# Which engine waits for the last store: TensorE or SyncE at the end of an add-and-GELU kernel

## The chip, the cores and the metric

The kernel runs on one core of one Trainium2 chip. The core has five engines, each with an instruction queue of its own: TensorE (PE in the profile), VectorE (DVE), ScalarE (ACT), GpSimd (POOL) and SyncE (SP). [...] The metric is the device time of one execution in microseconds (us); lower is better.

## The reference

The kernel adds two arrays of 1024 x 4096 float32 values and passes the sum through the tanh form of GELU:

```python
def reference(x, y):
    z = x + y
    return (0.5 * z * (1 + np.tanh(np.sqrt(2 / np.pi) * (z + 0.044715 * z ** 3)))).astype(np.float32)
```

It reads 33.55 MB and writes 16.78 MB.

## The kernel before, in words

Each of the 128 partitions holds 32,768 consecutive elements of x, y and the output. SyncE issues all transfers: four loads of x and four of y, of 8,192 elements a partition each, in turn (lines 129 and 136), and then three stores of 16,384, 10,240 and 6,144 elements a partition (line 140). The arithmetic runs in 16 chunks of 2,048 elements a partition. GpSimd adds x and y in all chunks but the first (line 153). ScalarE squares (line 158), VectorE forms the cubic term (line 164), ScalarE takes a sigmoid (line 169) and VectorE multiplies (line 176) into the tile that is stored. TensorE has no arithmetic at all. The order in each queue is written out by hand in four lists, and `tc.compile()` on line 231 adds waits, branches and the end of the program.

Two helpers then edit the compiled program. `begin_early` moves the first two loads ahead of the barrier at the start. `wait_late` edits the last block. As compiled, that block begins with SyncE waiting for everything that is outstanding; then comes a barrier of all five engines, then GpSimd clears the kernel's semaphores (line 50), then a second barrier. Each barrier is made of two semaphores, 96 and 97: every engine but GpSimd raises 96 in a DRAIN instruction, GpSimd waits for four of those, adds 4 to 97, and every other engine takes one off 97 in an EVENT_SEMAPHORE instruction. All of these instructions carry line 231 in the profile.

`wait_late` takes the wait for the last store (semaphore 103, which the last store raises to 32) out of SyncE's first wait. It leaves semaphore 103 out of GpSimd's clearing, by splitting the range in two, and appends one more EVENT_SEMAPHORE after the second barrier. That instruction waits until semaphore 103 is at least 32 and subtracts 32. In the kernel before it stands in SyncE's queue as its last instruction. So the barriers and the clearing run while the last store is still moving, and the program's own last instruction is SyncE's. Behind the last instruction of each queue follow instructions that are not the kernel's: they have no line in the profile, but the trace holds their updates of semaphores.

Of the kernel before, what the change touches and what calls it, by code (L numbers as in the profile page):

```python
# [25 lines left out]
def wait_late(nc):  # L26

    body, end = (b.instructions for b in nc.main_func.blocks[1:3])  # L30
    last = [i for i in body if isinstance(i, mybir.InstDMACopy)][-1]
    (sem,) = [u.id for u in last.sync_info.on_update]
    all_done = end[0]
    reset = next(i for i in end if isinstance(i, mybir.InstDrain) and i.is_reset_sema)
    at = end.index(reset)
    clear = end[at + 1]
    first, stop = reset.reset_range_start, reset.reset_range_stop
    assert all_done.engine == mybir.EngineType.SP and reset.engine == mybir.EngineType.Pool
    assert isinstance(clear, mybir.InstISA) and clear.engine == mybir.EngineType.Pool
    waits = all_done.sync_info.on_wait  # L40
    (its,) = [w for w in waits if w.id == sem]

    end[0] = mybir.InstDrain(
        name=all_done.name, engine=all_done.engine, debug=all_done.debug, is_reset_sema=False,
        sync_info=mybir.SyncInfo(on_wait=[w for w in waits if w.id != sem], on_update=[]),
    )
    parts = []
    for f, e in ((first, sem), (sem + 1, stop)):
        if f < e:
            nc.gpsimd.sem_clear(range(f, e))  # L50
            parts.append(nc.cur_bb.bb.instructions.pop())
    end[at + 1 : at + 2] = parts
    end.append(
        mybir.InstEventSemaphore(
            name=clear.name, engine=mybir.EngineType.SP, debug=clear.debug,
            sync_info=mybir.SyncInfo(
                on_wait=[its],
                on_update=[
                    mybir.SyncUpdate(
                        sync_type="semaphore", id=sem, ant_name=its.ant_name,  # L60
                        update_mode="sem-sub-imm", update_value=its.wait_value,
                    )
                ],
            ),
        )
    )
# [3 lines left out]
def kernel(  # L70
# [160 lines left out]
    tc.compile()  # L231
    begin_early(nc, 2)
    wait_late(nc)


# [28 lines left out]
```

## Time and profile before

| what | value |
|---|---|
| median of 3 runs | 120.31 us (120.29 to 120.6) |
| the profiled execution's own time | 120.49 us |
| span of the profile, first to last instruction of the kernel | 118.8 us (118.83) |
| time of the profiled execution outside the span | 1.66 us (120.49 - 118.83) |
| busy in the span | DVE 73.7 us, ACT 61.0 us, POOL 69.7 us, TensorE none |
| traffic | 50.33 MB, mean 424 GB/s over the span |
| last store issued by SyncE | starts at 106.9 us, 3,072 KB, 11.9 us to landing |
| the kernel's last instruction | SyncE's EVENT_SEMAPHORE, starts at 118.8 us, 17 ns |

Times within the profile count from the start of the span. A "q" behind an engine's name (SPq, POOLq) stands for instructions that its sequencer handles alone: waits, drains, issues of transfers. TensorE's appear as PEq or PEldq. Such instructions are not counted as busy. The duration shown for one of them mostly begins when its wait is over, so a short duration doesn't mean that it waited briefly.

### The profile page before, as it was taken

Reading aid. Unit: us, or ns where it says so; the run is one execution under the profiler, and the core shown is the slowest. Engines: PE = TensorE matmul, PEld = TensorE weight load, DVE = VectorE, ACT = ScalarE, POOL = GpSimd, SP = SyncE. Lnnn points to the kernel's source line nnn. Section 1 sums busy time; section 2 is a strip of 40 time slices with the busy share of each in tenths; the row PEclk is TensorE's granted clock in tenths of the full one; section 3 lists DMA queues with packets and bytes.
Section 4 is the critical chain, followed back from the end, with each engine's and each line's share of the span. In section 5 each row is a group of like instructions: output and inputs, shape, how many; then the busy total and the mean of one; then the engine's idle time right before and its main releaser. Section 6 shows DMA issues by size and latency. Waiting matters only on the chain.

```text
span 118.8 us, 172 instructions
## 1 busy us (share of the span) xinstructions
DVE 73.7 (62%) x35; ACT 61.0 (51%) x34; POOL 69.7 (59%) x19
## 2 busy tenths in 40 slices
DVE  0000000635799995739999968999994999990000
ACT  5000000063888965197698647888839779810000
POOL 0000000699996099999959999959999990000000
DMA  7989898989999898989899898998899889999996
GB/s 243 463 375 507 353 529 353 507 375 474 408 419 463 375 507 353 518 364 496 386 452 430 386 496 353 529 529 353 353 596 463 353 353 441 441 441 441 397 397 265
DMA packets 1584, 50.33 MB, mean 424 GB/s; under 512 B 176, under 2 KB 176, under 8 KB 176
## 3 DMA queue, kind: packets, MB, share of 16 engines
q1 hardware_dynamic: 1584, 50.33, 98.7%
HBM read 33.55 MB, written 16.78 MB: 424 GB/s over the span
## 4 chain that ended last, share of the span: by engine, by line
DMA 51%; POOL 26%; POOLq 4%; DVE 4%; DVEq 2%; ACT 2%; issue 0%; SPq 0%
DMA y<-in_y_dram 51%; POOL z L153 26%; POOLq L231 4%; DVE w L164 2%; DVEq L231 2%; DVE z L176 2%; ACT w L158 2%; SPq L129 0%; POOLq L153 0%
## 5 line engine op out<-in xcount | busy, mean ns | idle before, releaser
L153 POOL TENSOR_TENSOR z<-z,y 128x2048 f32<-128x2048 f32 x15 | 69.4, 4660 | 28.3 <-DMA y<-in_y_dram 28.3
L158 ACT ACTIVATE w<-z 128x2048 f32<-128x2048 f32 x16 | 30.1, 1882 | 37.7 <-DVE z L153 21.5
L164 DVE SCALAR_TENSOR_TENSOR w<-w,z 128x2048 f32<-128x2048 f32 x16 | 36.7, 2296 | 11.2 <-ACT w L158 11.0
L176 DVE TENSOR_TENSOR z<-w,z 128x2048 f32<-128x2048 f32 (+1 forms) x17 | 35.9, 2155 | 0.0
L169 ACT ACTIVATE w<-w 128x2048 f32<-128x2048 f32 x16 | 29.7, 1855 | 4.4 <-DVE w L164 4.3
L153 DVE TENSOR_TENSOR z<-z,y 128x2048 f32<-128x2048 f32 x1 | 2.3, 2293 | 20.5 <-DMA y<-in_y_dram 20.5
L216 ACT ACT_TABLE_LOAD x1 | 1.3, 1283 | 1.3 <-PEq L248 1.3
L215 DVE MEMSET one<- 128x1 f32 x1 | 0.1, 59 | 1.3 <-PEq L248 1.3
L248 POOL MEMSET const-float32-0.0<- 128x1 f32 x1 | 0.1, 98 | 0.2 <-issue 0.2
L216 ACT ACTIVATE one<-one 128x1 f32<-128x1 f32 x1 | 0.2, 203 | 0.0
L248 POOL MEMSET const-bfloat16-1.0<- 128x1 bf16 x1 | 0.1, 101 | 0.0
L248 POOL MEMSET const-uint8-127<- 128x1 uint8 x1 | 0.1, 101 | 0.0
L248 POOL MEMSET const-float32-1.0<- 128x1 f32 x1 | 0.1, 98 | 0.0
## 6 DMA issues: line engine op xcount, KB each, us to landing
z<-in_x_dram SPq DMA_DIRECT2D x4, 4096.0 KB, 31.4
y<-in_y_dram SPq DMA_DIRECT2D x4, 4096.0 KB, 22.2
out_dram<-z SPq DMA_DIRECT2D x1, 5120.0 KB, 15.8
out_dram<-z SPq DMA_DIRECT2D x1, 3072.0 KB, 11.9
out_dram<-z SPq DMA_DIRECT2D x1, 22.0
```

Source lines behind the costliest of these rows:

```text
L153: eng.tensor_add(out=zt[:, a:b], in0=zt[:, a:b], in1=yt[s][:, o : o + b - a])
L158: nc.scalar.activation(out=wt[c], in_=zt[:, a:b], func=act.Square, scale=root)
L164: nc.vector.scalar_tensor_tensor(out=wt[c], in0=wt[c], scalar=c1, in1=zt[:, a:b], op0=alu.add, op1=alu.mult)
L169: nc.scalar.activation(out=wt[c], in_=wt[c], func=act.Sigmoid)
L176: ins = nc.vector.tensor_mul(out=zt[:, a + o : a + o + n], in0=wt[c][:, o : o + n], in1=zt[:, a + o : a + o + n],)
L215: nc.vector.memset(one, 0.0)
L216: nc.scalar.activation(out=one, in_=one, func=act.Sigmoid)
L231: tc.compile()
L248: nc = _bacc.Bacc("TRN2", target_bir_lowering=False, num_devices=1)
```

## The change

The instruction that waits for semaphore 103 and subtracts 32 from it is placed in TensorE's queue and not in SyncE's. It stays the last instruction of the block, with the same wait and the same subtraction. SyncE's queue then ends with its step of the second barrier, and TensorE's queue has one instruction more behind its own step of that barrier. Nothing else differs: all loads, stores and arithmetic stand in the same order on every engine.

```diff
     end.append(
         mybir.InstEventSemaphore(
-            name=clear.name, engine=mybir.EngineType.SP, debug=clear.debug,
+            name=clear.name, engine=mybir.EngineType.PE, debug=clear.debug,
             sync_info=mybir.SyncInfo(
                 on_wait=[its],
                 on_update=[
```

## The prediction

> **What bounds the kernel now.** I first read the page's slices, to see what the stretch around the change is limited by:
>
> ```profile
> DVE  0000000635799995739999968999994999990000
> POOL 0000000699996099999959999959999990000000
> DMA  7989898989999898989899898998899889999996
> ```
>
> The DMA engines are busy from the first slice to the last, and no engine computes in the last four slices (from about 107 us). The end is the last store. SyncE's waits in the stretch from 107 us on say who waits for it:
>
> ```profile
> SPq L140 <- DVE z L176: 10.7, 1, 10.7
> SPq L231 <- SPq L231: 6.4, 1, 6.4
> SPq L231 <- DMA out_dram<-z: 4.2, 1, 4.2
> ```
>
> The columns are us in total, times and longest. The last store is issued after the last multiplication of VectorE (first row). SyncE then waits 4.2 us for the store before the last, passes both barriers, and waits 6.4 us more. The view puts this last wait down to SyncE itself, but the instruction waits for semaphore 103 alone, so it is the last store that ends it. Then I read what the instructions of line 231 cost each engine, in the view of that line for 110 to 119 us:
>
> ```profile
> L231 SPq EVENT_SEMAPHORE  x6: 17/22/4230, 107.3 to 118.8; - x6
> L231 ACTq EVENT_SEMAPHORE  x2: 17/17/17, 111.9 to 112.4; - x2
> L231 DVEq EVENT_SEMAPHORE  x2: 21/21/21, 111.9 to 112.4; - x2
> L231 PEldq EVENT_SEMAPHORE  x2: 51/51/51, 111.9 to 112.5; - x2
> ```
>
> The numbers after the count are shortest, median and longest in ns, then the first and last start. The reader should see two things. The same kind of instruction takes 17 ns on SyncE (its shortest, the moved one among them) and 51 ns on TensorE. And everything but SyncE's last instruction is over at 112.5 us, 6.3 us before the end at 118.8 us.
>
> The profile's instructions stop there, but 1.66 us of this execution's 120.49 lie outside its span, and the trace keeps updates of semaphores from them. Those of semaphore 2, in us from the start of the span, are:
>
> ```
> before the kernel   -0.374 -0.340 -0.302 -0.258 -0.235 | -0.123 -0.084 -0.050 -0.003
> first after it     112.736 112.770 112.975 113.019 118.971 | 119.015 119.053 119.087 119.135
> second after it    119.922 119.956 119.995 120.039 120.062 | 120.161 120.199 120.233 120.280
> ```
>
> Nine updates make one pass over the five engines, up and down again. In the first pass after the kernel, four updates are made long before the end, then nothing for 6 us, then the fifth 0.141 us after SyncE's last instruction. So SyncE is fifth, the turning point, and the other four have already taken their upward step when the store lands. The change removes this arrangement.
>
> [...] the second pass takes 120.280 - 119.922 = 0.358 us. [...]
>
> **Where TensorE stands in the pass.** No record names the engine of an update, so I infer it. Before the kernel the last update is at -0.003 us, and TensorE's first instruction is the last of all, at 0.312 us; VectorE, ScalarE and GpSimd begin between 0.119 and 0.131, SyncE at 0. In the reset between the two later passes, semaphores are cleared in groups of 51. The first group (3 to 53) ends last, at 119.698, at about 7.6 ns each even after the others are through, where the first clears of SyncE's group take about 1.5 ns each. The slow sequencer of the table above is TensorE's. I take TensorE as first in the pass: it goes up first and comes down last.
>
> **The change part by part.**
>
> Removed: SyncE's last instruction and what follows it up to the barrier. Semaphore 103 got its last increment at 118.796, the instruction began at 118.813 (17 ns later) and took 17, and SyncE's update came at 118.971. From the landing to the turning point: 118.971 - 118.796 = 0.175 us. From there down to the first engine: 119.135 - 118.971 = 0.164. Sum: 0.339 us.
>
> Added: the same instruction on TensorE.
> - Waking: in both barriers TensorE began 28 and 29 ns after semaphore 97 was raised, SyncE 17. I take 0.028.
> - Executing: 0.051, from the row above. Subtracting 32 and not 1 should cost the same: SyncE's last instruction takes 17 ns like its decrements.
> - From its last kernel instruction to its step in the pass: TensorE's last ended at 112.501, the first update came at 112.736: 0.235. SyncE needs 0.141. I take 0.235 unchanged. It could be less if some of it was waiting for others; I bound it from below by SyncE's 0.141.
> - The whole pass, since nobody can go up before TensorE: the second pass is a case of just that, with TensorE last out of its reset. It takes 0.358.
>
> Sum: 0.028 + 0.051 + 0.235 + 0.358 = 0.672 us from the landing to the end of the pass. Difference: 0.672 - 0.339 = **+0.333 us**. Nothing hides it: at that point no transfer and no arithmetic is left. From the pass on, reset and second pass follow as before: TensorE's reset was last before and is last again.
>
> Moved with it: nothing else. No DMA is issued in that block, and SyncE's three stores stand ahead of it in the same order. Queued behind the waiting instruction on TensorE is nothing of the kernel, only its part of the end sequence, and all other engines wait for that in the pass. SyncE passes 6.3 us earlier to its own step, where it waits for the other four; I cost that at nothing, since the pass is held by TensorE in any case. The GpSimd clearing, leaving out semaphore 103, is as before.
>
> So the span itself should grow hardly at all: the kernel's last instruction ends at 118.796 + 0.028 + 0.051 = 118.875 and not 118.830, +0.045 us. The time outside it should grow from 1.66 to about 1.66 + 0.29 = 1.95 us. For the profiled execution: 120.49 + 0.33 = 120.82. That one lies 0.18 above the median of the runs shown, within their 0.31 us of spread, so for the median: 120.31 + 0.33 = **120.64 us**, +0.28%.
>
> A measurement of this kernel can tell about 0.3% from no change, 0.36 us here, so the forecast lies just under what counts as slower.
>
> **Rivals.**
>
> The pass is dearer than the second one shows. In the first pass the third step came 112.975 - 112.770 = 0.205 us after the second, where the warm passes show 0.038 and 0.039. I read that as an engine that arrived late. But if it is what this step costs after a kernel (GpSimd's last kernel instruction had ended at 112.413, the earliest of all, which speaks for it), the path is longer by 0.205 - 0.039 = 0.166: +0.50 us, 120.81. If, beyond that, instructions that each engine runs ahead of its step come into the path one after the other, up to 0.14 us for each of the four behind TensorE, it is +0.333 + 0.56 = +0.89, 121.20. Against it: they had 6 us to run ahead. Slower is certain once over 0.03 us is added to my sum.
>
> TensorE isn't first in the pass, but second to fourth. Then one to three of the upward hops (0.034, 0.039 and 0.044) fall away: +0.333 - 0.034 = 0.30 to 0.333 - 0.117 = 0.22 us; with the lower bound of 0.141 for its way to the pass also 0.094 less: +0.12, 120.43. The slow group of semaphores speaks against it.
>
> The other side, no loss or a gain: the measured end doesn't hang on TensorE's passing the barrier but on SyncE's own end sequence, which now lies under the store. Then SyncE's 0.141 goes and only TensorE's 0.045 comes: 0.045 - 0.141 = -0.10 us, 120.21. It decides if the records after the landing show SyncE's group going on early. Against it: 6 us of silence in the pass before the change, and none of it is skipped.
>
> That the change does nothing (another wait ends last) can be excluded: the moved instruction is the last of the span, 6.3 us behind all others.
>
> **How the numbers follow.** TensorE first, pass as in the second: 0.64; with some 0.1 us of scatter in the runs around +0.333, it gives slower 0.29, same 0.34, faster 0.01. Dearer pass: 0.18, all slower. TensorE elsewhere: 0.12, same 0.11, faster 0.01. End sequence of SyncE: 0.06, same 0.04, faster 0.02. Sum: slower 0.47, same 0.49, faster 0.04. The range begins between the cases +0.12 and +0.22 less a little scatter (120.40) and reaches over the dearer pass at 120.81 and some way towards 121.20, to 121.00; about 0.1 is left out on each side.
>
> **What would show it.** In the profile after: a span of 118.9 us if the DMA part is the same, ending with a TensorE EVENT_SEMAPHORE of 51 ns; no update of semaphore 2 between the barriers at 112.5 us and the landing; then nine updates in a row, the first 0.31 us after the last increment of semaphore 103, the ninth 0.36 later. Wrong would be early updates (TensorE isn't first), a pass well over 0.36 us (the dearer pass), or a first pass as short as before.

## The result and the profile after

The changed kernel takes 120.72 us (median of 6 runs, 120.67 to 120.79), the kernel before 120.39 us (median of 6, 120.29 to 120.6). The ratio is 1.0027, 95% interval 1.0014 to 1.0039: 0.33 us more, between 0.17 and 0.47 us. The change costs time, since the whole interval lies above 1, but it stays just under the 0.3% that the prediction took as the bound of a clear loss.

The page of the changed kernel has the same picture in its slices as before: transfers to the end, nothing computed in the last four slices.

```profile
DVE  0000000635799995749999958999994999990000
POOL 0000000699996199999959999959999990000000
DMA  7999898989999898989899898998899889999896
```

SyncE's waits from 107 us on (us in total, times, longest):

```profile
SPq L140 <- DVE z L176: 10.7, 1, 10.7
SPq L231 <- DMA out_dram<-z: 4.3, 1, 4.3
SPq L231 <- PEq L231: 0.6, 2, 0.5
```

The row of 6.4 us that stood between the first two is gone: SyncE waits for nothing more after the second barrier. (The third row, its waits in the barriers, is the same in the kernel before.) The view of line 231 for 110 to 119 us shows where the instruction went (count, then shortest, median and longest in ns, then the first and last start):

```profile
L231 SPq EVENT_SEMAPHORE  x5: 17/28/4252, 107.2 to 112.3; - x5
L231 PEldq EVENT_SEMAPHORE  x3: 51/51/51, 111.8 to 118.7; - x3
L231 ACTq EVENT_SEMAPHORE  x2: 17/17/17, 111.8 to 112.3; - x2
```

SyncE's are one fewer and end at 112.3; TensorE has one more, at 118.7 us, and it takes 51 ns. That one ends the span, at 118.705 us. The span is no longer than before (118.83), although the time is. The difference lies outside the span, in the updates of semaphore 2 (us from the start of the span; semaphore 103 had its last increment at 118.625):

```
first after the kernel   118.984 119.018 119.056 119.100 119.124 | 119.222 119.261 119.295 119.342
second after it          120.129 120.164 120.202 120.246 120.269 | 120.368 120.406 120.440 120.487
```

Before, four of the nine steps of the first pass were taken 6 us ahead of the landing. Now the first comes 0.359 us after the landing, and the other eight follow it. In the profiled executions the pass ends 0.339 us after the landing before and 0.717 after: 0.378 us more. The time outside the span (the time of a run less its span, mean of all runs; spans are on record to 0.1 us) rose from 1.663 us (35 runs of the kernel before, made with E1 to E4 below) to 1.995 us (6 runs), by 0.332. The span itself has 0.046 us more of TensorE's waking and executing, which the scatter of the spans covers (118.6 to 119.5 us in those 35 runs). The two add up to the 0.378 us of the traces.

### The profile page after: what moved, and what is told of

Read it like the earlier page. It is cut to its first block, busy times and chain, and to the rows that moved or that the text cites. A ratio compares the mean times of both kernels' runs of the same rounds, so it can differ in the third digit from the quotient of the medians.

```text
span 118.7 us, 172 instructions
## 1 busy us (share of the span) xinstructions
DVE 73.7 (62%) x35; ACT 61.0 (51%) x34; POOL 69.6 (59%) x19
## 4 chain that ended last, share of the span: by engine, by line
DMA 51%; POOL 26%; POOLq 4%; DVE 4%; DVEq 2%; ACT 2%; issue 0%; SPq 0%
DMA y<-in_y_dram 51%; POOL z L153 26%; POOLq L231 4%; DVE w L164 2%; DVEq L231 2%; DVE z L176 2%; ACT w L158 2%; SPq L129 0%; POOLq L153 0%
```

## The experiments

The theory: after the landing, four things follow each other. The waiting engine wakes; it executes the instruction; it makes its own way to its step in the pass (the time from the end of its last kernel instruction to that step); then comes the rest of the pass behind that step. The rivals: only TensorE's slow sequencer costs, with 51 ns for the instruction that takes SyncE 17 (A); any engine but SyncE, the turning point, pays the same (B); the end depends on SyncE's own end sequence. Two properties of the traces served as gauges: the number of updates of semaphore 2 made ahead of the landing (4 with SyncE, 0 with TensorE) is read as the waiting engine's place, and the distances between events give each part in ns. The columns from "wakes" to "sum" are in ns, from the profiled executions; "sum" is the time from the landing to the end of the first pass. "Outside" is the mean of time less span over the runs, in us. The ratio of an experiment is to runs of the kernel before made in the same round; their "outside" was 1.663 us for E1 to E4, 1.671 for E5 to E8 and 1.668 for E9 to E12.

| kernel | early steps | wakes | executes | way | rest of pass | sum | outside | ratio to before, 95% interval |
|---|---|---|---|---|---|---|---|---|
| before (SyncE) | 4 | 17 | 17 | 141 | 164 | 339 | 1.663 | |
| after (TensorE) | 0 | 29 | 51 | 279 | 358 | 717 | 1.995 | 1.0027 [1.0014, 1.0039] |
| E1 ScalarE | 1 | 21 | 17 | 140 | 324 | 502 | 1.640 | 0.9998 [0.9988, 1.0009] |
| E2 VectorE | 3 | 28 | 21 | 183 | 242 | 474 | 1.790 | 1.0021 [1.0013, 1.0030] |
| E3 GpSimd | 2 | 24 | 17 | 561 | 286 | 888 | 2.200 | 1.0044 [1.0032, 1.0056] |
| E4 TensorE and 4 drains | 0 | 28 | 51 + 364 | 192 | 358 | 993 | 1.906 | 1.0064 [1.0052, 1.0076] |
| E5 SyncE, 4 drains on TensorE | 4 | 17 | 17 | 140 | 164 | 338 | 1.663 | 1.0001 [0.9994, 1.0009] |
| E6 TensorE, 4 drains on SyncE | 0 | 29 | 51 | 279 | 359 | 718 | 2.010 | 1.0033 [1.0021, 1.0045] |
| E7 SyncE and 4 drains | 4 | 17 | 17 + 232 | 120 | 163 | 549 | 1.643 | 1.0021 [1.0014, 1.0029] |

In E4 and E7 the four drains belong to the span, so "outside" alone doesn't show them; the sum does.

**E1 to E3: another engine waits.** The edit, here for ScalarE (VectorE is `DVE`, GpSimd `Pool`):

```diff
-            name=clear.name, engine=mybir.EngineType.PE, debug=clear.debug,
+            name=clear.name, engine=mybir.EngineType.Activation, debug=clear.debug,
```

> The wait for the last store stands on ScalarE. From the landing (last increment of semaphore 103) to the end of the first pass it was 0.339 us with SyncE waiting and 0.717 with TensorE. Theory (each engine pays waking, executing, its own way to its step, and the rest of the pass behind its step): ScalarE is second, so one early update of semaphore 2, and 0.02 + 0.017 + way + (0.358 - 0.034), the way between SyncE's 0.141 and the 0.311 that the trace of before allows: 0.50 to 0.67 us, 0.16 to 0.33 over before. Rival A (only TensorE's slow sequencer costs): as before, within 0.05 us. Rival B (every engine but the turning point pays alike): +0.33 to 0.38.

> The wait for the last store stands on VectorE. Theory (waking, executing, own way, rest of the pass): VectorE is fourth, so three early updates, and 0.027 + 0.021 + way + (0.358 - 0.117), [...]: 0.47 to 0.84 us, 0.13 to 0.50 over before, the low end likelier. Rival A (only TensorE's slow sequencer costs): as before, within 0.05 us. Rival B (all but the turning point pay alike): +0.33 to 0.38.

> The wait for the last store stands on GpSimd. Theory (waking, executing, own way, rest of the pass): GpSimd is third, so two early updates, and 0.024 + 0.017 + way + (0.358 - 0.072), the way between 0.141 and the 0.562 us from GpSimd's last kernel instruction (112.413) to the late third update of before (112.975). If that late update was GpSimd's own way, 0.89 us, 0.55 over before, more than TensorE although it stands later; if it was a dear hop of the pass, TensorE waiting would have shown it too, and its pass took 0.358. Low end 0.47, +0.13. Rival A (only TensorE's slow sequencer costs): as before, within 0.05. Rival B (all but the turning point pay alike): +0.33 to 0.38.

The early steps are 1, 3 and 2, with 0 for TensorE and 4 for SyncE: the pass goes TensorE, ScalarE, GpSimd, VectorE, SyncE. That settles the places that the prediction had to infer. That the four updates behind the fifth go back the same way is still a reading: no record names an update's engine. In E3 the updates of the first pass are, in us from the start of the span, with the landing at 118.643 and the end of GpSimd's instruction at 118.684:

```
first after the kernel   112.619 112.653 119.245 119.290 119.313 | 119.411 119.450 119.485 119.531
```

Two steps are taken early, and the third comes 561 ns after GpSimd's instruction. In the kernel before it came 562 ns after GpSimd's last instruction (112.975 - 112.413). That decides between the two readings of the late third step there: it is GpSimd's own way, not a dear hop. So GpSimd costs 0.549 us over before by the trace and 0.53 us (0.39 to 0.67) in the runs, more than TensorE although it stands two places later. In the view of line 231 its instruction is no slower than SyncE's (first row before, second row E3):

```profile
L231 POOLq EVENT_SEMAPHORE  x4: 17/17/17, 111.8 to 112.4; - x4
L231 POOLq EVENT_SEMAPHORE  x5: 17/17/17, 111.7 to 118.7; - x5
```

The reader should see that the second row alone would have suggested a cost like SyncE's; what costs is behind the last instruction of the profile. A falls with VectorE and GpSimd, B with the spread from 0.135 (VectorE) to 0.549 us (GpSimd) by the trace. The low end of 0.47 us expected for VectorE was the author's estimate; the trace has 0.474. For VectorE the trace gives 0.135 us more than before, and outside the span the runs have 0.127; the ratio has slightly more, 0.16 to 0.36 us, the rest of it in spans that were 0.06 us longer on average. ScalarE doesn't fit: its trace gives 0.163 us more, its runs show no difference, and even the upper end of the interval, 0.11 us, is below. So for ScalarE the theory has the path right and the time wrong. E9 to E12 are about that.

**E4 to E7: four drains more, on the engine that waits and on one that doesn't.** The edit, here for TensorE, behind the last instruction of the changed kernel (E4) or of the kernel before (E5); with `SP` it gives E6 and E7:

```diff
+    more = [
+        mybir.InstDrain(
+            name=nc.get_next_instruction_name(), engine=mybir.EngineType.PE, debug=clear.debug,
+            is_reset_sema=False,
+            sync_info=mybir.SyncInfo(on_wait=[], on_update=[]),
+        )
+        for k in range(4)
+    ]
+    end.extend(more)
```

> The changed kernel with four DRAIN instructions more on TensorE behind the wait. Theory (all that TensorE has behind the wait is on the path, one after the other): a DRAIN takes 8 ns and began 100 ns after the instruction ahead of it, so 4 x 0.108 = 0.43 us more than the changed kernel: 0.717 + 0.43 = 1.15 us from the landing to the end of the pass, and 0.8 us (0.65%) over before. Rival (what is behind the wait is fetched and run ahead, only the wait itself counts): as the changed kernel, 0.717 and +0.3%.

> The kernel before (SyncE waits) with four DRAIN instructions more at the end of TensorE's queue. Theory (TensorE's way to its step lies under the store there): TensorE's step comes 0.43 us later, at about 113.2 us from the start of the span, 5.6 us ahead of the landing; from the landing to the end of the pass 0.339 us as before, time as before within 0.05 us. Rival (TensorE's end sequence counts wherever the wait stands): +0.4 us, +0.35%.

> The changed kernel with four DRAIN instructions more at the end of SyncE's queue. Theory: SyncE's way to its step is now under the store: as the changed kernel, 0.717 us from the landing to the end of the pass, +0.3% on before. Rival (SyncE's end sequence sets the end by itself): 4 x 0.055 = 0.22 us more, +0.5% on before.

> The kernel before with four DRAIN instructions more on SyncE behind the wait. Theory: SyncE's way is on the path there: a DRAIN of 7 ns with some 48 ns ahead of it, 4 x 0.055 = 0.22 us more, 0.56 us from the landing to the end of the pass, +0.18% on before. Rival (only TensorE's end sequence sets the end): as before.

The drains lengthen the path when they stand behind the wait on the waiting engine (E4: +0.276 us over the changed kernel; E7: +0.210 us over before) and cost nothing on an engine that doesn't wait (E5 and E6: 0.001 us or less by the traces). The rows of TensorE's drains in the changed kernel (first) and in E4, in which the added lines move 231 to 240:

```profile
L231 PEldq DRAIN  x1: 8/8/8, 112.0 to 112.0; - x1
L240 PEldq DRAIN  x5: 8/8/8, 112.1 to 119.2; - x5
L240 PEldq EVENT_SEMAPHORE  x3: 51/51/51, 112.0 to 118.8; - x3
```

Four drains of 8 ns take 364 ns, from the end of the wait to the end of the last: the time is between instructions, not in them. E4 stayed under the 0.43 us expected, since the drains began 116, 72 and 68 ns apart, not 108, and the way behind them shrank from 279 to 192 ns. The rival that what is behind the wait runs ahead is refuted by E4. That TensorE's end sequence counts wherever the wait stands is refuted by E5, that SyncE's sets the end by itself by E6, and that only TensorE's counts by E7.

**E8: one drain on TensorE, for its way.** The block above with `range(1)`, in the kernel before.

> The kernel before with one DRAIN more at the end of TensorE's queue, for what makes TensorE's way to its step 0.279 us with the change where it was 0.235 before. If one instruction more in TensorE's queue shifts what follows, the way from the end of the DRAIN to the first update is about 0.28; if it is the long wait, or the kind of the last instruction, about 0.235. The time as before.

One run: 120.37 us; the path from the landing is 339 ns as before. TensorE's way from the end of the drain to its step is 243 ns, much nearer to 235 than to 279: one instruction more in the queue doesn't by itself make 279. Behind four drains the way is 192 ns, with the long wait ahead of them (E4) and without it (E5), so it depends on what stands ahead of it. What sets it is open.

**E9 to E12: what is different on ScalarE.** For all kernels of the table above but E1, "outside" is the end of the first pass less the end of the last instruction (before: 0.339 - 0.034 = 0.305 us) plus 1.353 to 1.372 us. For E1 this remainder is only 1.640 - (0.502 - 0.038) = 1.176 us. The question is what takes 0.18 us off it. The edit is the block above with `Activation` for `PE`: one drain (E9) or four (E10) in the kernel before, one in the kernel of E1 (E11), one in the changed kernel (E12).

> The kernel before with one DRAIN more at the end of ScalarE's queue, under the last store. With ScalarE waiting, the trace put the end of the pass 0.163 us later than before, yet the time outside the span was 1.640 us a run, 0.18 less than the trace of that kernel gives by the rule that held for all others (end of the pass less end of the last instruction, plus 1.36). Theory C (what stands behind the kernel on ScalarE changes when its queue is one instruction longer, wherever the wait is): about 1.48 us outside the span where the kernel before has 1.666, and 0.15% faster. Theory D (it hangs on ScalarE being the one that is held): 1.666, time as before.

> The same with four DRAINs on ScalarE. Theory C: again about 1.48 us outside the span, or some other value than 1.666, if it hangs on where the queue ends. Theory D: 1.666, time as before, since the DRAINs run under the last store.

> ScalarE waits, with one DRAIN more behind the wait. The path from the landing to the end of the pass grows by one DRAIN, some 0.06 us, to 0.56. Theory C: the time outside the span still 0.18 below the rule, 0.56 - 0.09 + 1.18 = 1.65 us, if it is the longer queue of ScalarE. Theory D: the same, if it is the holding of ScalarE. A value by the rule (1.83) would say that the one queue length was what mattered.

> The changed kernel (TensorE waits) with one DRAIN more at the end of ScalarE's queue. Theory C: 1.995 - 0.18 = 1.81 us outside the span, 0.13% over before and not 0.27%. Theory D: 1.995, +0.3% as the changed kernel. From the landing to the end of the pass 0.717 in both.

| kernel | sum, ns | outside, us | outside less the part up to the end of the pass, us | ratio to before, 95% interval |
|---|---|---|---|---|
| E1 ScalarE waits | 502 | 1.640 | 1.176 | 0.9998 [0.9988, 1.0009] |
| E9 SyncE waits, 1 drain on ScalarE | 339 | 1.486 | 1.180 | 0.9976 [0.9964, 0.9988] |
| E10 SyncE waits, 4 drains on ScalarE | 338 | 1.556 | 1.250 | 0.9987 [0.9974, 1.0000] |
| E11 ScalarE waits, 1 drain behind | 540 | 1.461 | 1.020 | 0.9984 [0.9973, 0.9995] |
| E12 TensorE waits, 1 drain on ScalarE | 717 | 1.818 | 1.181 | 1.0013 [0.9997, 1.0029] |

One instruction more in ScalarE's queue takes 0.18 us off the time, whichever engine waits (E1, E9, E12): that the effect goes with ScalarE's queue (theory C) holds, that it takes ScalarE being held by the wait (D) falls. The cost of the change is the same with this drain in both kernels: 1.818 - 1.486 = 0.332 us outside the span. C's number was missed in E11: two more (one of them the wait) take off 0.34, where I had expected 1.65 us outside. Four take off 0.11 on average, and there the runs scatter from 1.28 to 1.67 us. So the effect doesn't grow with the number of instructions. The other engines show nothing like it: with one instruction more on TensorE (the change), VectorE (E2) or GpSimd (E3) the remainder is 1.358, 1.365 and 1.353 us, and 1.358 in the kernel before.

The drain itself is an 8 ns row. ScalarE's drains from 110 us on in the kernel before (first row), and E9's view:

```profile
L231 ACTq DRAIN  x1: 14/14/14, 112.0 to 112.0; - x1
L240 SPq EVENT_SEMAPHORE  x6: 17/22/4252, 107.5 to 119.0; - x6
L240 ACTq DRAIN  x2: 8/11/14, 112.2 to 112.7; - x2
```

It runs at 112.7 us, 6 us before SyncE's last wait ends, so nothing on the path within the span moved. E9 has the lowest median of all kernels here, 120.23 us against 120.42 before.

Why the time gets shorter is open. In E9 the path from the landing to the end of the first pass is as before, 0.339 us. Its second pass is longer (us from the start of the span):

```
second after the kernel   120.065 120.099 120.137 120.181 120.205 | 120.303 120.341 120.511 120.558
```

The eighth step, ScalarE's if the pass goes back as it came, comes 0.170 us after the seventh where it was 0.034. E1 and E12 have the same late step (0.170 and 0.157 us), E10 and E11 don't. From the end of the span to the last update of semaphore 2 it is 1.747 us in E1, 1.584 in E9, 1.582 in E11 and 1.900 in E12. In each of them that is 0.08 to 0.12 us more than the whole time outside the span. For E8 and all other kernels of the first table it is 0.21 to 0.23 us less. So in these four kernels the measured time ends ahead of that last update, or it starts behind the first instruction of the span. The trace shows neither its start nor its end. Counted from the last update, the four are alike, some 0.3 us shorter than the others, and the 0.18 us of E1, E9 and E12 differ from the 0.34 us of E11 by about what the late step adds. That is a reckoning from one trace of each kernel, not an experiment. E10's trace has a transfer of 8,192 bytes of instructions at 120.05 us, within the second pass; no other trace has one behind the kernel. That may go with its scatter, but was not tried.

## Why the prediction was right, step by step

- *TensorE stands first.* Right. It rested on who starts last and on the slow group of semaphores, and on the author's reading of the nine updates as one pass over the five engines; that no step of the changed kernel is early, and the early steps of E1 to E3, show it directly. The rival in which TensorE stands second to fourth is refuted.
- *Waking 0.028, executing 0.051.* Right: 0.029 and 0.051. Subtracting 32 costs TensorE what subtracting 1 does, 51 ns.
- *The way to the pass, 0.235 us taken unchanged.* Mis-sized: 0.279 us with the change. The whole difference between the sum of the prediction (0.672 us from the landing) and the trace (0.717) is this 0.044 and 0.001 of waking. The bound from below (0.141) was on the wrong side. E8, E4 and E5 show 0.243 and 0.192 behind drains, so the value isn't a constant of the engine.
- *The whole pass, 0.358 us as in the second pass.* Right to the ns: 0.358 again. The last kernel instructions of all others had ended by 112.36 us, 6.3 us before the landing. The dearer pass, the rival that held 0.18 of the 0.47 given to "slower", read the late third step of before as a possible price of the hop. E3 shows that it was GpSimd arriving, 561 ns after its last instruction. The far end of that rival (+0.89 us) also has a sum that leaves something out: it is said to come beyond the dear hop, but without that hop's 0.166 us. With it, it would be 1.06 us.
- *The drop of 0.339 us on SyncE, and SyncE's earlier arrival at nothing.* Right: E5 and E6 show that four drains more at the end of TensorE's or SyncE's queue cost nothing when that engine doesn't wait (0.001 us or less by the traces), E4 and E7 that they count when it does (0.276 and 0.210 us).
- *The gain by SyncE's end sequence.* Refuted by the silence of the pass until TensorE's step, 0.359 us after the landing, and by E6 (718 ns against 717).
- *The span.* The prediction had +0.045 us for the end of the span behind the landing; the trace has 0.080 against 0.034. Outside it, it had about 1.95 us, and the runs have 1.995.

So the forecast of +0.333 us met a measured +0.33 (0.17 to 0.47), while the trace's own sum is +0.378 us. The nearness of the first two is partly luck of the scatter. The forecast of the time itself, 120.64 us, was 0.08 us under the measured 120.72, because the median of the kernel before was 120.39 us over six runs and not 120.31.

What the prediction missed is not on its path: it had no term for what a longer queue does off the path. E9 shows that one instruction more at the end of ScalarE's queue is worth 0.18 us, about half of the change itself. TensorE's queue, one instruction longer after the change, has no such effect: the remainder is 1.358 us in both kernels, and E5 and E8, with four and one more on TensorE, show none either (1.663 and, in one run, 1.67 us outside). Had the wait been moved to ScalarE, the same working would have forecast some 0.16 us too much.

## What to carry to other kernels

Here the last instruction of the kernel wasn't the end of its time: 1.663 us before and 1.995 us after the change lay outside the span. Where one wait ends last, look at what its engine still has to do behind it: in the semaphore updates behind the span, not in the instruction's own duration. By the traces the way from the landing to the end of the first pass was shortest with SyncE, 0.339 us, then came VectorE, ScalarE, TensorE and GpSimd at 0.474, 0.502, 0.717 and 0.888. Then measure the time as well: with ScalarE waiting it was the same as with SyncE (0.9998), 0.163 us less than the updates said. To see whether something is on such a path, lengthen it on purpose: four drains on the waiting TensorE or SyncE counted (0.276 and 0.210 us by the traces); the same four on the other of the two cost nothing (0.001 us or less).

## What the runs showed of the hardware that was not expected

- In this kernel, after the same wait, the way from an engine's last instruction to its step in the first pass was 0.14 us for SyncE (before) and ScalarE (E1), 0.18 for VectorE (E2), 0.28 for TensorE (after) and 0.56 for GpSimd (E3).
- TensorE's drains of 8 ns began 68 to 116 ns apart, SyncE's of 7 ns 52 to 57 ns apart (E4 and E7).
- One drain more at the end of ScalarE's queue, under the last store, made the kernel 0.24% faster (0.9976, interval 0.9964 to 0.9988), with 0.18 us less outside the span. No like effect was seen with one instruction more on TensorE, VectorE or GpSimd: the remainder was 1.358, 1.365 and 1.353 us, and 1.358 before. The cause is open.
